# Two 64-row score products side by side, other head loads, and small moves in a decoder block's kernel

## The chip, the cores and the metric

The kernel runs on one core of one Trainium2 chip. The metric is the device time of one execution in microseconds (us); lower is better. It is a single launch with all arrays in the chip's memory; the largest part of the work is matrix products on TensorE (PE), with VectorE (DVE), ScalarE (ACT) and GpSimd (POOL) around it and transfers issued by SyncE (SP) and POOL.

## The reference

One decoder block with 1024 positions, width 1024 and FFN width 2816, in float32:

```python
h = rmsnorm(x, attn_norm_g)
z = h @ w_in                                  # u,v | pooled | q | k | v
gates = sigmoid(h @ w_gate + b_gate)          # three times 1024 columns
y_a = gmlp_mixer(z[..., :512])                # 256 wide
y_b = pool_mixer(z[..., 512:768])             # 256 wide
y_c = diff_attn_mixer(q, k, v, ...)           # 4 heads, values 128 wide
merged = g_a * (y_a @ proj_a) + g_b * (y_b @ proj_b) + g_c * (y_c @ proj_c)
x = x + merged @ w_out
x = x + conv_ffn(rmsnorm(x, ffn_norm_g), w_up, conv_w, conv_b, w_down)
return rmsnorm(x, final_norm_g)
```

The differential attention has, for each of its 4 heads, two maps with 64-wide queries and keys and one 128-wide value:

```python
s = einsum('bqhcd,bkhcd->bhcqk', qi, k) * scale + bias   # c: the two maps, d = 64
s = where(rel >= 0, s, -1e30)
p = softmax(s)
a = p[:, :, 0] - lam * p[:, :, 1]
o = einsum('bhqk,bkhd->bqhd', a, v)
```

## The kernel before

**Products.** Nearly every large product is made from operands split into a high and a low part (`hi`, `lo`, both fp32r), in three passes: hi x hi, hi x lo, lo x hi (`mm3`, L191, over `PASSES`). The projections, the output projection (`strassen_full`, in six products p = 0 to 5) and the FFN use a scheme of the Strassen and Winograd kind, which has fewer products and more additions (L262, L235, L888 and others on DVE).

**Order.** The program is written in stages, and generators (`filler`, `avs`, `nxt`, `lates`) are stepped by hand in the attention's main loop. A scheduler then orders each engine's instructions by their place in the program and by its own estimate of time; each engine runs its list in that order. Buffers come from pools: `wp` (`w4`, 13 buffers of 512 KB), `ap_` (`a4`, 34 buffers), `cp` (`c2`, 6 of half the size), and banks of PSUM from rings of 3 (scores, `score_bank`), 2 (`pat`), 1 (`pms`) and 2 (`pmm`).

**Stages in time.** x and the u and v columns to 55 us, values and pooling to 105, q and k to 195, twelve gate pairs to 430 and a last q and k pair to 446; then the attention to 592, the third merge to 632, the output projection to about 715, the FFN's norm and its first products to 765, its up part to 1120, its down part to 1380.

**Attention.** Each head has 8 query tiles of 128 rows, 32 steps in all; tile i needs the first (i + 1) x 128 keys, in chunks of at most 512. `store_qk` writes the split q and k of a head to memory (`qk_d`), `load_head` brings a head back: for each map c a buffer `qs` with the 64 rows of q's high part over the 64 rows of its low part, and `kh` and `kl`, each with the same 64 rows twice. `scores(t, c)` does one map: for each chunk one product of 128 rows with `kh` (L759) and one with `kl` (L760), which together are the passes hi x hi, lo x hi, hi x lo (and lo x lo); then DVE adds the bias and takes the row minimum (L762) and ACT takes the exponential (L768) with the minimum as bias. `transpose` (L1103), `attend` (L1112) and `sub_norm` (L1140) follow a few steps later. Between them stands filler: `merge_ab` (the merges of the first two mixers, L1146 for their weights `pr`, split into `ph`; L1165 and L1166 for the gates) and `merge_c`.

**Around it.** In the output projection `wfull` (L843) and `wh` (L835) load weights `fr`, DVE makes sums of them (L888), ACT and DVE split them into `fw` (L96, L97), ACT copies x (L912), and the result goes to memory at L1020. For the FFN's norm `rms4a` sums squares and takes a root by `rsqrt` on ACT (L123, a table has to be loaded for it) with one Newton step on DVE, `rms4b` broadcasts it. L390 makes the relative bias: it is the one place of the trunk where products use fewer than 128 rows (33).

Of the kernel before, what the change touches and what calls it, by code (L numbers as in the profile page):

```python
# [18 lines left out]
P = 128  # L19
# [3 lines left out]
NH = 512  # L23
# [24 lines left out]
def trunk_kernel(  # L48
# [446 lines left out]
    v_d = dram.tile([8, P, NH], F32, name="v_d")  # L495
# [6 lines left out]
    def values():  # L502
# [32 lines left out]
        def store(o, banks, c, r, i):  # L535

            for b in range(2):
                TT(out=o[b], in0=banks[b], in1=c[b], op=ALU.add)
                for t in range(2):
# [3 lines left out]
                nc.sync.dma_start(out=v_d[tt:tt + 2, :, r * 256:(r + 1) * 256].rearrange("t p c -> p t c"),  # L543
                                  in_=o[b].rearrange("p (t c) -> p t c", t=2))
# [132 lines left out]
    def store_qk(i, Fs, eng=None):  # L677
        for n_, F in enumerate(Fs):
# [6 lines left out]
            nc.sync.dma_start(out=qk_d[4 * n_ + i, 0], in_=hi.bitcast(F32))  # L685
            nc.sync.dma_start(out=qk_d[4 * n_ + i, 1], in_=lo.bitcast(F32))
# [20 lines left out]
    def load_head(hd):  # L707

        H = heads[hd] = dict(qkl=[])
# [15 lines left out]
        nc.sync.dma_start(out=H["V"], in_=v_d[:, :, hd * P:(hd + 1) * P].rearrange("t p c -> p t c"))  # L725
# [13 lines left out]
    def scores(t, c):  # L739
# [6 lines left out]
        if c == 0:  # L746
            if W <= NH:
                b = a4([P, 2, NH], n="sc")
                st[t] = dict(pr=[b[:, 0, :], b[:, 1, :]], s=[])
            else:  # L750
                st[t] = dict(pr=[a4(n="sc"), a4(n="sc")], s=[])
        q, kh, kl = H["qkl"][c]
        sc_ = st[t]["pr"][c]
        mx = tiny(2, "mx")
        chunks = [(0, min(NH, W))] + ([(NH, W - NH)] if W > NH else [])
        for n_, (c0, n) in enumerate(chunks):
            ps = score_bank[0]()
            qs = q[:, i * P:(i + 1) * P]
            nc.tensor.matmul(ps[:, :n], lhsT=qs, rhs=kh[:, c0:c0 + n], start=True, stop=False)  # L759
            nc.tensor.matmul(ps[:, :n], lhsT=qs, rhs=kl[:, c0:c0 + n], start=False, stop=True)  # L760
            o = (7 - i) * P + c0
            nc.vector.tensor_tensor_reduce(  # L762
                out=sc_[:, c0:c0 + n], in0=ps[:, :n], in1=H["T"][:, o:o + n], scale=1.0,
                scalar=mx[:, 0:1] if n_ else 3.0e38,
                op0=ALU.add, op1=ALU.min, accum_out=mx[:, n_:n_ + 1])
        nm_ = mx[:, n_:n_ + 1]
        sum_ = H["s0"][:, i:i + 1] if c == 0 else tiny(1, "s1")
        nc.scalar.activation(out=sc_[:, :W], in_=sc_[:, :W], func=AF.Exp, bias=nm_, scale=-1.0, accum_out=sum_)  # L768
        st[t]["s"].append(sum_)
# [39 lines left out]
    def strassen_full(src, w, nsl, x_d, out, done, tail=None, LL=4):  # L809
# [30 lines left out]
        def wfull(p, j):  # L840
            if (p, j) not in halves:
                t = w4(n="fr")
# [160 lines left out]
    tprep = [], []  # L1003
# [9 lines left out]
    def done1(d, j):  # L1013
# [47 lines left out]
        if (d // 4, j) == (1, 0):  # L1061
            tprep[1].append(t4)
# [14 lines left out]
    score_bank[0], pat, pms, pmm = pt2("sc", 3), pt2("at", 2), pt2("ms", 1), pt2("mm", 2)  # L1077
# [132 lines left out]
    mc = merge_c([pmm, pmm, *score_bank * 3, pat, pat])  # L1210
    lates = []
    for t in range(len(tiles) + 3):
        hd, i = tiles[min(t, 31)]
        if t == 0:
            yab = [load_yab(i) for i in range(4)]
        if t == 2:
            store_qk(NHEAD - 1, last_qk)
        if t % 8 == 3 and t < 24:
# [318 lines left out]
```

## Time and profile before

| | us |
|---|---|
| median of 3 runs | 1384.76 |
| lowest and highest run | 1382.77, 1390.9 |
| the profiled execution's own time | 1389.13 |
| its span in the trace | 1387.4 |
| its mean granted TensorE clock | 0.991 of full speed |

The profile records one execution of the program: every instruction of each engine with start and end, what it waited for, and every transfer. It is 4.4 us slower than the median of the runs, and its own time is 1.7 us more than its span. A matmul's recorded end is modelled, so the pace of PE is read from start to start. Engines other than PE have idle time that need not matter; what counts is where PE waits.

### The profile page before, as it was taken

Reading aid. Unit: us, or ns where it says so; the run is one execution under the profiler, and the core shown is the slowest. Engines: PE = TensorE matmul, PEld = TensorE weight load, DVE = VectorE, ACT = ScalarE, POOL = GpSimd, SP = SyncE. Lnnn points to the kernel's source line nnn. Section 1 sums busy time; section 2 is a strip of 40 time slices with the busy share of each in tenths; the row PEclk is TensorE's granted clock in tenths of the full one; section 3 lists DMA queues with packets and bytes.
Section 4 is the critical chain, followed back from the end, with each engine's and each line's share of the span. In section 5 each row is a group of like instructions: output and inputs, shape, how many; then the busy total and the mean of one; then the engine's idle time right before and its main releaser. Section 6 shows DMA issues by size and latency. Waiting matters only on the chain.

```text
span 1387.4 us, 17666 instructions
## 1 busy us (share of the span) xinstructions
PE 1344.9 (97%) x6454; PEld 1120.5 (81%) x6454; DVE 964.5 (70%) x1487; ACT 652.4 (47%) x1109; POOL 495.9 (36%) x327
## 2 busy tenths in 40 slices
PE   9999999999999989999999999999999999999997
PEld 7997778888887778877777888888888887878786
DVE  7985774445444879958769576666777669985853
ACT  8633343344433666723667343433343435455461
POOL 0022334455553000022221665666656640102014
PEclk9999999999999999999999999999999999999998
DMA  7023363333239898588795222212222248845853
GB/s 261 10 78 109 108 222 134 121 121 104 101 115 272 252 242 209 151 233 193 201 221 131 83 77 91 79 74 91 91 77 91 75 151 305 274 126 150 226 128 122
DMA packets 78831, 204.65 MB, mean 148 GB/s; under 512 B 8270, under 2 KB 17614, under 8 KB 78744
## 3 DMA queue, kind: packets, MB, share of 16 engines
q1 hardware_dynamic: 67224, 180.44, 39.4%
q0 software_dynamic: 11520, 23.07, 9.7%
q8 instruction: 51, 0.84, 0.2%
q14 instruction: 36, 0.29, 0.1%
HBM read 143.70 MB, written 47.46 MB: 138 GB/s over the span
## 4 chain that ended last, share of the span: by engine, by line
PE 67%; DVE 13%; DMA 10%; issue 6%; ACT 3%; POOL 1%; SPq 1%; DVEq 0%; POOLq 0%; ACTq 0%
PE b L191 59%; PE mm L191 2%; DMA fr<-in_w_down 2%; DMA pr<-in_w_proj 1%; DVE ft L97 1%; PE ms L1112 1%; DVE fw L97 1%; DMA qs<-qk_d 1%; POOL ga L104 1%; DMA fr<-in_w_out 1%; DVE sc L762 1%; DMA x<-in_xT 1%; DMA yr<-y_d 1%; PE sc L759 1%; ACT fw L96 1%
## 5 line engine op out<-in xcount | busy, mean ns | idle before, releaser
L191 PE MATMUL b<-ft,fw 128*128 128x512 f32 (+1 forms) x1308 | 293.0, 384 | 9.8 <-ACT x L912 3.4
L191 PEld LDWEIGHTS b<-ft,fw 128*128 128x128 f32 x1308 | 239.9, 189 | 60.3 <-DVE fw L97 4.0
L354 POOL TENSOR_TENSOR F<-F,RB 128x1024 f32<-128x1024 f32 x68 | 185.5, 2730 | 111.3 <-DVE F L262 110.2
L262 DVE TENSOR_TENSOR F<-b,c 128x512 f32<-128x512 f32 x152 | 100.9, 683 | 130.5 <-ACT c L281 58.3
L191 PE MATMUL b<-hb,Ah 128*128 128x512 f32 x608 | 190.2, 392 | 0.0
L191 PE MATMUL b<-T,Sh 128*128 128x512 f32 x504 | 155.8, 390 | 1.9 <-ACT c L272 1.9
L234 POOL TENSOR_TENSOR s<-r 128x512 f32<-128x512 f32 x36 | 54.4, 1512 | 224.3 <-DMA r<-in_w_up 84.2
L191 PEld LDWEIGHTS b<-hb,Ah 128*128 128x128 f32 x608 | 114.5, 189 | 24.0 <-issue 0.5
L191 PE MATMUL b<-hb,Al 128*128 128x512 f32 x304 | 119.5, 393 | 2.5 <-DVE Al L97 2.5
L97 DVE TENSOR_TENSOR Al<-r,Ah 128x1024 fp32r<-128x1024 f32 x38 | 56.1, 1476 | 94.0 <-issue 77.9
L97 DVE TENSOR_TENSOR Sl<-s,Sh 128x1024 fp32r<-128x1024 f32 x76 | 107.0, 1408 | 13.9 <-ACT Sh L96 8.5
L96 ACT CAST Sh<-s 128x1024 fp32r<-128x1024 f32 x76 | 80.0, 1052 | 75.6 <-PE b L191 43.2
L191 PEld LDWEIGHTS b<-T,Sh 128*128 128x128 f32 x504 | 94.6, 188 | 21.8 <-ACT c L272 2.4
L191 PE MATMUL b<-T,Sl 128*128 128x512 f32 x252 | 98.1, 389 | 0.0
L191 PE MATMUL b<-hb,Sh 128*128 128x512 f32 x304 | 94.1, 391 | 2.9 <-DVE F L262 2.9
L96 ACT CAST Ah<-r 128x1024 fp32r<-128x1024 f32 x38 | 39.9, 1049 | 110.9 <-PE b L191 104.0
L96 ACT CAST fw<-fr 128x512 fp32r<-128x512 f32 x90 | 54.8, 622 | 62.4 <-DVE fw L97 25.0
L191 PE MATMUL b<-Th,Sh 128*128 128x512 f32 x204 | 79.1, 391 | 0.8 <-ACT c L267 0.8
L191 PE MATMUL b<-Tl,Sh 128*128 128x512 f32 x204 | 79.5, 390 | 0.0
L191 PE MATMUL b<-Th,Sl 128*128 128x512 f32 x204 | 79.4, 389 | 0.0
L191 PEld LDWEIGHTS b<-hb,Sh 128*128 128x128 f32 x304 | 56.8, 188 | 16.6 <-DVE F L262 4.2
L191 PEld LDWEIGHTS b<-hb,Al 128*128 128x128 f32 x304 | 57.4, 189 | 15.3 <-DVE Al L97 2.9
(284 smaller groups left out, 2838.9 us busy)
## 6 DMA issues: line engine op xcount, KB each, us to landing
fr<-in_w_down SPq DMA_DIRECT2D x47, 512.0 KB, 3.8
r<-in_w_up SPq DMA_DIRECT2D x42, 512.0 KB, 3.5
r<-in_w_gate SPq DMA_DIRECT2D x24, 512.0 KB, 3.6
g_d<-F SPq DMA_DIRECT2D x24, 512.0 KB, 2.8
act_d<-cv SPq DMA_DIRECT2D x22, 512.0 KB, 2.8
act<-act_d SPq DMA_DIRECT2D x22, 512.0 KB, 7.8
fr<-in_w_out SPq DMA_DIRECT2D x18, 512.0 KB, 6.1
ssb<-sq POOLq DMA_DIRECT2D x24, 256.0 KB, 4.1
```

What stands on the lines that cost most here:

```text
L96: nc.scalar.copy(hi, src)
L97: (eng or nc.vector).tensor_tensor(out=lo, in0=src, in1=hi.bitcast(F32), op=ALU.subtract)
L104: nc.gpsimd.dma_start(out=dst, in_=src, accum_op=ALU.add)
L191: last_mm[0] = nc.tensor.matmul(ps, lhsT=w[a], rhs=x[b], start=first and i == 0, stop=last and i == 2, skip_group_check=more)
L234: eng.tensor_tensor(out=s1[:, :NH], in0=a21, in1=a22, op=ALU.add)
L262: nc.vector.tensor_tensor(out=o, in0=ps, in1=c, op=ALU.add)
L354: (eng or nc.gpsimd).tensor_tensor(out=F, in0=F, in1=RB, op=ALU.mult)
L759: nc.tensor.matmul(ps[:, :n], lhsT=qs, rhs=kh[:, c0:c0 + n], start=True, stop=False)
L762: nc.vector.tensor_tensor_reduce(out=sc_[:, c0:c0 + n], in0=ps[:, :n], in1=H["T"][:, o:o + n], scale=1.0, scalar=mx[:, 0:1] if n_ else 3.0e38,
L1112: nc.tensor.matmul(po[:, :P], lhsT=AH[t][:, kb, :], rhs=H["V"][:, kb, :], start=kb == 0, stop=kb == i)
```

## The change

It does these things:

- `scores(t, n_)` is called by chunk instead of by map. For a chunk it takes two score banks and writes, for each of the three passes, one product of 64 rows for each map: map 0 on the array's rows 0 to 63, map 1 on rows 64 to 127. There are 288 score products instead of 192. The bias, the minima and the exponentials stay as many. In the main loop both chunks stand one after the other ahead of the filler. Score banks become 4, `pmm` 1; `sub_norm`'s transposes use score banks.
- `load_head` loads q and k for both maps as they lie in memory (4 transfers of 128 x 1024), and V from rows that are now contiguous for a head; values are stored in that layout in twice as many transfers. A head's load starts one step later in each group of eight. The last head's `store_qk` moves from step 2 to step 5 and to POOL's queue. The filler starts at step 0, with the first merge's operands ahead of the y loads.
- `wfull` takes a buffer of the `a4` pool for product p = 3 of the output projection.
- For the FFN's norm, the four sums of squares that were called through `tprep` are called in `rms_mid`, both roots ahead of both broadcasts; the root is taken on DVE with three Newton steps and no operation on ACT.

```diff
-    def rms4a(sq, pool):
+    def rms4a(sq, pool, act=True):
...
-        return rsqrt(t, 4)
+        return rsqrt(t, 4, act)
...
-    v_d = dram.tile([8, P, NH], F32, name="v_d")
+    v_d = dram.tile([NHEAD, P, 8, P], F32, name="v_d")
...
-                nc.sync.dma_start(out=v_d[tt:tt + 2, :, r * 256:(r + 1) * 256].rearrange("t p c -> p t c"),
-                                  in_=o[b].rearrange("p (t c) -> p t c", t=2))
+                for k in range(2):
+                    nc.sync.dma_start(out=v_d[2 * r + k, :, tt:tt + 2, :],
+                                      in_=o[b].rearrange("p (t k c) -> p k t c", t=2, k=2)[:, k])
...
-    def store_qk(i, Fs, eng=None):
+    def store_qk(i, Fs, eng=None, queue=nc.sync):
...
-            q, kh, kl = (a4(dt=F32R, n=n) for n in ("qs", "kh", "kl"))
-            r = slice(64 * c, 64 * c + 64)
-            for dst, src in ((q[0:64], qk_d[hd, 0, r]), (q[64:128], qk_d[hd, 1, r]),
-                             (kh[0:64], qk_d[4 + hd, 0, r]), (kh[64:128], qk_d[4 + hd, 0, r]),
-                             (kl[0:64], qk_d[4 + hd, 1, r]), (kl[64:128], qk_d[4 + hd, 1, r])):
-                nc.sync.dma_start(out=dst.bitcast(F32), in_=src)
-            H["qkl"].append((q, kh, kl))
+            q, k = a4(dt=F32R, n="q"), a4(dt=F32R, n="k")
+            nc.sync.dma_start(out=q.bitcast(F32), in_=qk_d[hd, c])
+            nc.sync.dma_start(out=k.bitcast(F32), in_=qk_d[4 + hd, c])
+            H["q"].append(q)
+            H["k"].append(k)
...
-        nc.sync.dma_start(out=H["V"], in_=v_d[:, :, hd * P:(hd + 1) * P].rearrange("t p c -> p t c"))
+        nc.sync.dma_start(out=H["V"], in_=v_d[hd])
...
-        for n_, (c0, n) in enumerate(chunks):
-            ps = score_bank[0]()
-            qs = q[:, i * P:(i + 1) * P]
-            nc.tensor.matmul(ps[:, :n], lhsT=qs, rhs=kh[:, c0:c0 + n], start=True, stop=False)
-            nc.tensor.matmul(ps[:, :n], lhsT=qs, rhs=kl[:, c0:c0 + n], start=False, stop=True)
-            o = (7 - i) * P + c0
+        ps = [score_bank[0]() for _ in range(2)]
+        for k, (a, b) in enumerate(PASSES):
+            for c in range(2):
+                r = slice(64 * c, 64 * c + 64)
+                nc.tensor.matmul(ps[c][:, :n], lhsT=H["q"][a][r, i * P:(i + 1) * P], rhs=H["k"][b][r, c0:c0 + n],
+                                 start=k == 0, stop=k == 2)
...
-                t = w4(n="fr")
+
+                t = a4(n="fr") if p == 3 and nsl <= 4 else w4(n="fr")
...
-            tprep[1].append(t4)
+            t4s.append(t4)
...
-    score_bank[0], pat, pms, pmm = pt2("sc", 3), pt2("at", 2), pt2("ms", 1), pt2("mm", 2)
+    score_bank[0], pat, pms, pmm = pt2("sc", 4), pt2("at", 2), pt2("ms", 1), pt2("mm", 1)
...
-        if t == 2:
-            store_qk(NHEAD - 1, last_qk)
-        if t % 8 == 3 and t < 24:
+        if t == 5:
+            store_qk(NHEAD - 1, last_qk, queue=nc.gpsimd)
+        if t % 8 == 4 and t < 24:
             nxt = load_head(hd + 1)
-        if t % 8 >= 3:
+        if t % 8 >= 4:
             next(nxt, None)
         if t:
             scores(t, 0)
+            scores(t, 1)
         transpose(t - 2, 0)
         next(avs, None)
-        if t >= 1:
-            next(filler, None)
-        scores(t, 1)
+        next(filler, None)
+        if t == 0:
+            scores(t, 1)
...
     def rms_mid():
+        for n_, j in enumerate((1, 0)):
+            for f in t4s[2 * n_:2 * n_ + 2]:
+                f()
+            rs[j] = rms4a(stat[j], pb3, False)
+            yield
         for j in (1, 0):
-            rs[j] = rms4a(stat[j], pb3)
-            yield
             rms4b(rs[j], half(j), pb3)
             yield
```

The three places that follow show what stands in an engine's list before and after. The first is PE in the attention. `sc` is a score bank, `kh`, `kl` and `k` are moving keys, `qs` and `q` stationary queries; the numbers tell buffers apart. Before:

```order
L759 MATMUL sc_4118<-kh_3845,qs_3844 128x512
L760 MATMUL sc_4118<-kl_3846,qs_3844 128x512
L1112 MATMUL ms_4104<-V_3550,ah_4050 128x128 x4
L759 MATMUL sc_4122<-kh_3845,qs_3844 128x384
L760 MATMUL sc_4122<-kl_3846,qs_3844 128x384
L759 MATMUL sc_4138<-kh_3766,qs_3765 128x512
L760 MATMUL sc_4138<-kl_3767,qs_3765 128x512
L191 MATMUL mm_4109<-yv_3626,ph_4014 128x512
```
After, the same stage; `sc_4167` is the bank of map 0 and `sc_4168` that of map 1, and the two `k` and `q` are high and low parts:

```order
L191 MATMUL mm_4001<-yv_3641,ph_3755 128x512
L761 MATMUL sc_4167<-k_3843,q_3842 128x512
L761 MATMUL sc_4167<-k_3913,q_3842 128x512
L761 MATMUL sc_4167<-k_3843,q_3912 128x512
L761 MATMUL sc_4168<-k_3843,q_3842 128x512
L761 MATMUL sc_4168<-k_3913,q_3842 128x512
L761 MATMUL sc_4168<-k_3843,q_3912 128x512
L1118 MATMUL ms_4143<-V_3548,ah_4086 128x128 x4
L761 MATMUL sc_4177<-k_3843,q_3842 128x256
L761 MATMUL sc_4177<-k_3913,q_3842 128x256
L761 MATMUL sc_4177<-k_3843,q_3912 128x256
```
Where two products per map stood, three stand, and the maps come one after the other rather than in turns. In the list of after 36 of 48 chunks stand so; 11 stand in turns and one in part. One that stands in turns, the first chunk of the attention:

```order
L761 MATMUL sc_3665<-k_3524,q_3523 128x512
L761 MATMUL sc_3666<-k_3524,q_3523 128x512
L761 MATMUL sc_3665<-k_3530,q_3523 128x512
L761 MATMUL sc_3666<-k_3530,q_3523 128x512
L761 MATMUL sc_3665<-k_3524,q_3529 128x512
L761 MATMUL sc_3666<-k_3524,q_3529 128x512
```
Counted over the whole list, a product on one half of the rows stands next to one on the other half 66 times: 36 of 512 columns, 8 of 384, 13 of 256 and 9 of 128. The score products stand in 54 separate runs with other products between them; before there were 60 such runs, of which 37 followed an fp32 product (L1103, L1112) and 23 one of L191.

The second place is SP's list at the loading of the second head. Before:

```order
L716 DMA qs_3765<-qk_d 64x1024 x2
L716 DMA kh_3766<-qk_d 64x1024 x2
L716 DMA kl_3767<-qk_d 64x1024 x2
L722 DMA T_3774<-fsc 128x1024
L1165 DMA ga_3800<-g_d 128x1024
L1166 DMA gb_3801<-g_d 128x1024
L716 DMA qs_3844<-qk_d 64x1024 x2
L716 DMA kh_3845<-qk_d 64x1024 x2
L716 DMA kl_3846<-qk_d 64x1024 x2
L725 DMA V_3902<-v_d 128x8x128
L1165 DMA ga_4010<-g_d 128x1024
L1166 DMA gb_4011<-g_d 128x1024
L1146 DMA pr_4012<-in_w_proj 128x512
```
After:

```order
L713 DMA q_3842<-qk_d 128x1024
L714 DMA k_3843<-qk_d 128x1024
L721 DMA T_3846<-fsc 128x1024
L713 DMA q_3912<-qk_d 128x1024
L714 DMA k_3913<-qk_d 128x1024
L724 DMA V_3964<-v_d 128x1024
L1152 DMA pr_3994<-in_w_proj 128x512
```
The load has five transfers and V where there were thirteen and V, in larger pieces, and the gates' loads (`ga`, `gb`) no longer stand inside it; the projection weight `pr` comes right behind V in both.

The third is SP's list at the output projection, with product 3's weights at the `128x1024` rows and product 5's at `128x2x512`. Before:

```order
L843 DMA fr_6004<-in_w_out 128x1024
L843 DMA fr_6058<-in_w_out 128x1024
L1020 DMA x_d<-x_553_3611 128x512
L1020 DMA x_d<-x_554_3612 128x512
L1020 DMA x_d<-x_555_3613 128x512
L1020 DMA x_d<-x_556_3614 128x512
L843 DMA fr_6109<-in_w_out 128x1024
L843 DMA fr_6149<-in_w_out 128x1024
L835 DMA fr_6197<-in_w_out 128x2x512
L835 DMA fr_6245<-in_w_out 128x2x512
```
After:

```order
L849 DMA fr_6068<-in_w_out 128x1024
L1026 DMA x_d<-x_552_3611 128x512
L849 DMA fr_6122<-in_w_out 128x1024
L1026 DMA x_d<-x_553_3612 128x512
L849 DMA fr_6173<-in_w_out 128x1024
L1026 DMA x_d<-x_554_3613 128x512
L849 DMA fr_6213<-in_w_out 128x1024
L1026 DMA x_d<-x_555_3614 128x512
L840 DMA fr_6261<-in_w_out 128x2x512
```
Product 3's weights now stand between the stores of `x_d` instead of behind all four of them; the first of product 5's still stand behind.

## Rows read from the trace of the kernel before

**Rows 1.** The page: the span, and part 1, busy time of each engine.

```profile
span 1387.4 us, 17666 instructions
...
PE 1344.9 (97%) x6454; PEld 1120.5 (81%) x6454; DVE 964.5 (70%) x1487; ACT 652.4 (47%) x1109; POOL 495.9 (36%) x327
```

**Rows 2.** Windows: length; busy PE, PEld, DVE, ACT, POOL; clock, DMA share, GB/s.

```profile
446.70:500.00 53.30, 45.40 (x241) 36.80 (x241) 42.23 (x116) 31.81 (x85) 5.15 (x4) 0.94 0.94 269
500.00:592.00 92.00, 90.45 (x586) 79.35 (x584) 84.33 (x286) 65.53 (x202) 4.30 (x5) 1.00 0.76 191
```

**Rows 3.** Waits of PE, 440 to 600: total, times, longest.

```profile
PE mm L191 <- ACT ph L96: 3.3, 1, 3.3
PE sc L759 <- DVE mx L762: 2.5, 4, 1.5
PE sc L760 <- DMA kl<-qk_d: 1.6, 1, 1.6
```

**Rows 4.** Windows of 4 and 10 us, columns as in rows 2.

```profile
452.00:456.00 4.00, 4.00 (x12) 3.18 (x12) 4.00 (x11) 4.00 (x7) 0.37 (x1) 0.57 0.13 54
...
492.00:496.00 4.00, 2.63 (x7) 2.25 (x8) 2.13 (x8) 3.30 (x9) 0.00 (x0) 0.66 1.03 231
...
688.00:692.00 4.00, 3.62 (x10) 2.92 (x11) 1.95 (x3) 4.00 (x9) 3.25 (x5) 0.59 0.78 199
...
750.00:760.00 10.00, 8.19 (x40) 6.53 (x39) 10.00 (x18) 6.24 (x12) 2.18 (x3) 1.00 0.45 78
```

**Rows 5.** Matmuls of L759: ns min/median/max, first and last start, forms.

```profile
L759 PE MATMUL sc<-kh,qs x94: 220/389/522, 446.8 to 585.3; 128*128 128x512 f32 x46, 128*128 128x384 f32 x16, 128*128 128x256 f32 x16, 128*128 128x128 f32 x16
```

**Rows 6.** Timeline of PE, scores: start us, us, line, output and inputs.

```profile
480.75 0.39 PE L759 MATMUL sc<-kh,qs 128*128 128x512 f32 x1
...
481.43 0.39 PE L760 MATMUL sc<-kl,qs 128*128 128x512 f32 x1
...
488.99 0.42 PE L759 MATMUL sc<-kh,qs 128*128 128x384 f32 x1
489.25 0.34 PE L760 MATMUL sc<-kl,qs 128*128 128x384 f32 x1
489.42 0.39 PE L759 MATMUL sc<-kh,qs 128*128 128x512 f32 x1
...
507.89 0.28 PE L760 MATMUL sc<-kl,qs 128*128 128x128 f32 x1
508.00 0.34 PE L759 MATMUL sc<-kh,qs 128*128 128x256 f32 x1
...
508.29 0.28 PE L759 MATMUL sc<-kh,qs 128*128 128x256 f32 x1
508.41 0.28 PE L760 MATMUL sc<-kl,qs 128*128 128x256 f32 x1
```

**Rows 7.** Timeline of PE around L390 (33 rows), and its weight load behind.

```profile
130.32 0.39 PE L191 MATMUL b<-hb,Al 128*128 128x512 f32 x1
130.64 1.02 PE L390 MATMUL m<-oh,rb 33*4 33x512 f32 x2
131.59 0.73 PE L191 MATMUL b<-hb,Sh 128*128 128x512 f32 x2
132.15 0.40 PE L191 MATMUL b<-hb,Sl 128*128 128x512 f32 x1
...
131.59 0.30 PEld L191 LDWEIGHTS b<-hb,Sh 128*128 128x128 f32 x2 [0.86 <-issue]
```

**Rows 8.** Output projection: PE in the timeline; SP among the waits, 640 to 700.

```profile
688.38 2.08 PE L191 MATMUL b<-ft,fw 128*128 128x512 f32 x4 [3.36 <-ACT x L912]
...
SPq L835 <- DVE fw L97: 13.3, 3, 6.2
```

**Rows 9.** Timeline about the FFN norm: ACT and PE.

```profile
757.17 1.28 ACT L123 ACT_TABLE_LOAD   x1
...
760.14 0.73 PE L191 MATMUL b<-T,Sh 128*128 128x512 f32 x2 [1.95 <-ACT c L272]
```

More of the change, by code (lines that the diff above doesn't have):

```diff
@@ L684, in store_qk @@
                                            op0=ALU.mult, op1=ALU.subtract)
-            nc.sync.dma_start(out=qk_d[4 * n_ + i, 0], in_=hi.bitcast(F32))
-            nc.sync.dma_start(out=qk_d[4 * n_ + i, 1], in_=lo.bitcast(F32))
+            queue.dma_start(out=qk_d[4 * n_ + i, 0], in_=hi.bitcast(F32))
+            queue.dma_start(out=qk_d[4 * n_ + i, 1], in_=lo.bitcast(F32))
     def pool_outs():
@@ L707, in load_head @@
     def load_head(hd):
[L709 removed]
+        H = heads[hd] = dict(q=[], k=[])
         for c in range(2):
[L711 to L717 removed]
+            q, k = a4(dt=F32R, n="q"), a4(dt=F32R, n="k")
[3 more added lines that the diff above has]
+            H["k"].append(k)
             if c == 0:
@@ L737, in trunk_kernel, with scores @@
     score_bank = [pm1]
-    def scores(t, c):
+    def scores(t, n_):
         if t >= len(tiles):
@@ L745, in scores @@
         W = (i + 1) * P
-        if c == 0:
+        c0 = n_ * NH
+        n = min(NH, W - c0)
+        if n <= 0:
+            return
+        if n_ == 0:
+            st[t] = dict(s=[], mx=[tiny(2, "mx", 6) for _ in range(2)])
             if W <= NH:
                 b = a4([P, 2, NH], n="sc")
-                st[t] = dict(pr=[b[:, 0, :], b[:, 1, :]], s=[])
+                st[t]["pr"] = [b[:, 0, :], b[:, 1, :]]
             else:
-                st[t] = dict(pr=[a4(n="sc"), a4(n="sc")], s=[])
@@ L752, in scores @@
[L752 to L755, printed above, removed]
-        for n_, (c0, n) in enumerate(chunks):
-            ps = score_bank[0]()
-            qs = q[:, i * P:(i + 1) * P]
-            nc.tensor.matmul(ps[:, :n], lhsT=qs, rhs=kh[:, c0:c0 + n], start=True, stop=False)
-            nc.tensor.matmul(ps[:, :n], lhsT=qs, rhs=kl[:, c0:c0 + n], start=False, stop=True)
-            o = (7 - i) * P + c0
+                st[t]["pr"] = [a4(n="sc"), a4(n="sc")]
@@ L762, in scores @@
+        ps = [score_bank[0]() for _ in range(2)]
[4 more added lines that the diff above has]
+                                 start=k == 0, stop=k == 2)
+        o = (7 - i) * P + c0
+        for c in range(2):
+            sc_, mx = st[t]["pr"][c], st[t]["mx"][c]
             nc.vector.tensor_tensor_reduce(
-                out=sc_[:, c0:c0 + n], in0=ps[:, :n], in1=H["T"][:, o:o + n], scale=1.0,
+                out=sc_[:, c0:c0 + n], in0=ps[c][:, :n], in1=H["T"][:, o:o + n], scale=1.0,
@@ L764, in scores @@
                 scalar=mx[:, 0:1] if n_ else 3.0e38,
                 op0=ALU.add, op1=ALU.min, accum_out=mx[:, n_:n_ + 1])
[L766 to L769, printed above, removed]
+            if c0 + n == W:
+                sum_ = H["s0"][:, i:i + 1] if c == 0 else tiny(1, "s1")
+                nc.scalar.activation(out=sc_[:, :W], in_=sc_[:, :W], func=AF.Exp, bias=mx[:, n_:n_ + 1], scale=-1.0,
+                                     accum_out=sum_)
+                st[t]["s"].append(sum_)
@@ L1002, in trunk_kernel @@
     nc.scalar.mul(ngain, cs[:, C_GF:C_GF + KT], -1.0)
-    tprep = [], []
+    tprep, t4s = ([], []), []
     def op_g(src, g, n):
@@ L1209, in trunk_kernel @@
     LL = 4
-    mc = merge_c([pmm, pmm, *score_bank * 3, pat, pat])
+    mc = merge_c([pmm, *score_bank * 4, pat, pat])
     lates = []
@@ L1234, in trunk_kernel @@
         if u >= 0 and u % 8 == 7 and u < 31:
-            lates.append(sub_norm(tiles[u][0], (0, 1), pmm))
+            lates.append(sub_norm(tiles[u][0], (0, 1), score_bank[0]))
         if u == 27:
-            lates.append(sub_norm(3, (1,), pmm))
+            lates.append(sub_norm(3, (1,), score_bank[0]))
         if 0 <= t - 2 < 32:
```

1 line of the change is left out of this document (added).

## The prediction

> **What bounds the kernel now.** I read part 1 of the page first: PE is busy 1344.9 of 1387.4 us [rows 1]. So nearly everything that adds work to PE adds time, and other engines matter only where PE waits for them. The windows then say where PE has slack. In the first part of the attention (446.7 to 500) PE is busy 45.40 of 53.30 us at a mean clock of 0.94; in the rest of it (500 to 592) 90.45 of 92.00, at full clock [rows 2]. The waits name the idle time of the first part: 3.3 us for ACT's split of a projection weight (ph L96), 2.5 us for DVE's row minima (mx L762), 1.6 us for a half of a head that is still being loaded (kl<-qk_d) [rows 3]. The DMA share there is 1.03 in 492 to 496 [rows 4]: the queue engines are full, so the weights that ACT splits are late because the loads of a head stand in front of them. Twice in this part, and once in the output projection, PE's granted clock falls: 0.57, 0.66 and 0.59 of full speed in windows of 4 us [rows 4], the latter two right behind waits of 3.3 and 3.36 us [rows 3, 8]. At the lower of the two levels (1.2 instead of 2.4 GHz) a mean of 0.57 over 4 us is about 3.4 us of half pace, which loses 1.7 us.
>
> **A. The score products themselves.** L759 ran 96 times (94 in the row, and two under another bank's name) and L760 as often: per map and chunk one product each, 48 of 512 columns and 16 each of 384, 256 and 128 [rows 5]. From start to start they take 0.2265 us for 512 columns (480.75 to 481.43, three products), 0.17 for 384 (489.25 to 489.42), 0.12 for 256 (508.29 to 508.41) and 0.11 for 128 (507.89 to 508.00) [rows 6]. That is 2 x (48 x 0.2265 + 16 x 0.17 + 16 x 0.12 + 16 x 0.11) = 34.5 us.
> The change needs three products per map and chunk where two did, since hi and lo of q no longer stand over each other: 288 for 192. Had they to run one after another: 34.5 x 1.5 = 51.8, or +17.3. Were each product hidden beside one of the other map: 51.8 / 2 = 25.9, or -8.6. Which of the two is decided by who is whose neighbour. The built order shows that the maps seldom alternate: of 48 chunks 36 stand as three passes of one map and then three of the other, because the second map's bank is waited for, and only 11 alternate, one more in part. PE is taken to start them in the order in which they stand; then a product can lie beside another only if that one uses the other 64 rows and stands next to it, and there are 66 such pairs of neighbours (36 of 512, 8 of 384, 13 of 256, 9 of 128): 36 x 0.2265 + 8 x 0.17 + 13 x 0.12 + 9 x 0.11 = 12.1 us hidden at best. So 51.8 - 12.1 = 39.7: **+5**, bounds -8.6 and +17.3.
>
> **B. The array's shape.** Before, all the attention's products use 128 rows. Now 54 separate runs of score products of 64 rows stand between products of 128 rows, and each enters and leaves another shape of the array. One place in the trace shows such a change: L390, 33 rows among L191's 128 [rows 7]. The last product before it starts at 130.32 and L390 at 130.64, 0.32 later, where 0.226 is the pace: 0.09 lost on entering. Its two products start at 130.64 and, with 0.427 each in that pace (their 1.02 less the pipeline's 0.16), the last one ends its streaming at about 131.50. The first L191 that streams normally stands at 132.15, the third of its run, so the run would have begun at 132.15 - 2 x 0.226 = 131.70; its weight load started only at 131.59, after PEld had idled 0.86, instead of beside the product before. That is 0.21 on leaving; together 0.30 per run, 54 x 0.30 = 16.2. Of the old 60 runs 37 come from an fp32 group, and the first product then takes 0.26 until the next where 0.17 is the pace (488.99 to 489.25 to 489.42) [rows 6]: 37 x 0.085 = 3.1 that is paid already. Net **+13**, an estimate from one place with another row count; bounds 0 (a change of shape that no weight load has to wait for) and +18.
> The Trainium skill says so too ("TensorEngine Tiling (Array Packing)", Key Properties): to change the tiling mode drains TensorE. The row agrees, with 0.30 per run; the page gives no figure for it. The same page lets tiles on different rows work in parallel and prices a contraction of 64 at up to two times (Theoretical Speedup); by that price A would be -8.6 and the sum -7, where the order and the row make it +7. No row of before shows two products at once.
>
> **C. Waits of the attention's first part.** A head is now loaded by 5 large transfers and V, 3 MB in place of 4 (k is no longer loaded twice), from whole rows; it starts one step later in each group of eight. The last head's store moves from step 2 to step 5 and from SP's queue to POOL's, where nothing in this part is waited for. With a quarter of a head's bytes gone and head 1's V ahead of the third projection weight as before, that weight's wait (3.3) and the low clock behind it (1.7) should go, and the wait for kl (1.6): -6.6. The four waits for the minima (2.5) and the first low-clock stretch (1.7) may go with the fourth score bank and with filler from step 0: -10.8 at the outside. The mm bank that is given up costs little, since the merge products take turns with scores. I take **-7**, bounds 0 (the weight is late all the same) and -11.
>
> **D. The output projection.** PE waits 3.36 us at 688.38 for ACT's x, and SP stood 13.3 us behind DVE for w4 buffers [rows 8]: loads of w_out come late because the few w4 buffers are still held by splits. Product 3's loads now use the larger a4 pool, and in the order four of them move ahead of or between the x1 stores. But product 5's loads still stand after the stores and still take w4. The wait and its low-clock stretch are 3.4 + 1.7 = 5; I take **-4**, bound 0.
>
> **E. The FFN norm's root.** The ACT table load of 1.28 us (757.17) goes, and with it a cause of PE's 1.95 us wait for ACT's c at 760.14 [rows 9]. In its place DVE gets nine small operations of some 0.17 us in a stretch where it is busy 10.00 of 10 us [rows 4], ahead of the broadcast that PE waits for. The T4 product's sums are called elsewhere in the code but stand where they stood on DVE. **0**, bounds -2 and +1.5.
>
> **F. The rest.** V's store takes 16 transfers with 512-byte pieces in place of 8 with 1 KB, while the qk products keep PE busy; the load of V gets whole rows of 4 KB. 0 to +1 if the smaller pieces delay weights; taken at nothing. ab(0) ahead of the y loads is hidden behind the last gate pair.
>
> **Sum:** +5 +13 -7 -4 = +7 on the profiled execution's 1389.13, thus 1396; that execution stands 4.4 above the median of the runs, so **1392 us**, with 1385 to 1399 as this case's own range (B between 0.2 and 0.4 per run, C and D between half and all).
>
> **Rivals.**
> 1. The shape changes cost next to nothing. A run of K = 64 might load its weights ahead as others do; L390 has 33 rows and 4 columns, and is one place. Then +5 -7 -4, up to -10 with all of C and D whole (5 - 11 - 5 = -11): 1374 to 1379. It decides from under 0.1 us per run. For it: PE is 97% busy with PEld at 81% [rows 1], so weights are loaded beside products everywhere else. Against it: PEld's 0.86 of idleness in [rows 7]. I put 1376 (1368 to 1381).
> 2. No product lies beside another at all: +17.3 with B and the gains, 17 + 13 - 11 = +19: 1404. For it: no row of before shows two products at once. Against it: nothing but that the two halves share neither rows nor banks.
> 3. The maps do run side by side in spite of the order, because a product may begin on its rows as soon as these are free: -8.6, with a small B and the gains: 1366. Against it: the three passes of one map come first, and the other's bank is waited for.
> This kernel's runs spread from 1382.8 to 1390.9, so under 0.5% (6.9 us) counts as no change.
>
> **How the numbers follow.** Forecast 0.42, rival 1 0.30, rival 2 0.18, rival 3 0.10. Faster is under 1377.8: rival 3 whole, some 0.8 of rival 1: 0.34. Slower is over 1391.7: rival 2 and half of the forecast: 0.39. Same: the rest, 0.27. The range is 1364 to 1406, from rival 3 to rival 2's middle.
>
> **What would show it.** B: the scores' first product and the first L191 or fp32 product behind a run lie more than 0.2 us beyond the pace, with PEld idle ahead of them. A: products of the other map start much sooner than 0.2 us after their neighbour, 66 times; if more, rival 3. C: no wait for ph and no window under 0.9 clock in 480 to 500. D: the L912 wait is under 1 us. It would be wrong if PE's idle time inside 500 to 592, now 1.55 us, grew: then the bank waits have become the bound.

## The result and the profile after

The changed kernel takes 1397.78 us (median of 6 runs, 1394.22 to 1400.07), the kernel before 1385.49 (6 runs): a ratio of 1.0087, 95% interval 1.0069 to 1.0105, so 12 us slower. The profiled execution of after took 1397.29, at its median; the one of before (1389.13) lay 3.6 above its own. The two traces therefore differ by 8.2 us of span only, and a cause worth 4 us can't be read from them alone. Of these 8.2 us 2.9 lie ahead of the attention: the first score product of all starts at 436.67 before and at 439.53 after (timeline of PE, before and then after):

```profile
436.67 0.39 PE L759 MATMUL m<-kh,qs 128*128 128x512 f32 x1
```

```profile
439.53 0.50 PE L761 MATMUL m<-k,q 64*128 64x512 f32 x2
```

Some 1.7 of them (0.28 x 6) are a stretch at the lower clock. Windows of before and then after, columns as in [rows 2]:

```profile
84.00:90.00 6.00, 5.94 (x48) 5.91 (x49) 4.20 (x5) 2.88 (x5) 0.00 (x0) 1.00 0.00 0
```

```profile
84.00:90.00 6.00, 5.34 (x32) 5.34 (x33) 3.06 (x4) 0.80 (x2) 0.00 (x0) 0.72 0.00 0
```

In the same window the experiment e3 below has 0.72 too and e8 1.00, though both share with after all that runs there. So this stretch comes and goes with the execution and is no part of the change's price.

The page of after, its span and part 1, beside [rows 1]:

```profile
span 1395.6 us, 17830 instructions
...
PE 1358.9 (97%) x6550; PEld 1120.4 (80%) x6550; DVE 968.0 (69%) x1499; ACT 651.8 (47%) x1106; POOL 501.0 (36%) x331
```

PE is busy 14 us longer, and the span grew by 8.2: PE's work rose, and some of its waits went. Windows of after, columns as in [rows 2]:

```profile
446.70:500.00 53.30, 51.07 (x309) 38.19 (x310) 50.38 (x141) 38.12 (x96) 9.27 (x8) 1.00 0.87 294
500.00:592.00 92.00, 92.00 (x587) 71.44 (x586) 76.19 (x248) 58.66 (x179) 4.36 (x5) 1.00 0.48 141
642.00:692.00 50.00, 44.58 (x189) 36.47 (x188) 44.13 (x73) 25.60 (x46) 10.58 (x12) 0.93 0.78 200
770.00:776.00 6.00, 4.44 (x17) 3.97 (x18) 5.16 (x15) 0.59 (x1) 2.54 (x2) 0.72 0.24 97
```

The first part of the attention is now 51.07 of 53.30 us busy, at full clock: it was 45.40 at 0.94. The second part is full. But the clock is 0.93 in 642 to 692, 0.07 x 50 x 2 = 7 us at the lower level, and low again at 770 to 776. The waits of PE, 440 to 780, say why (total, times, longest):

```profile
PE b L191 <- DVE gc L1210: 5.4, 1, 5.4
PE b L146 <- DVE rs L131: 2.5, 1, 2.5
...
PE at L1109 <- DVE sc L1094: 0.7, 1, 0.7
```

All of [rows 3] is gone, and so are the waits of PE for ACT's x and for ACT's c in [rows 8, 9]. In their place stand 5.4 us at the start of the output projection, for the last products of the third merge that DVE has yet to take out of their banks (gc), and 2.5 us at the FFN norm's broadcast, for its root on DVE. The score products, beside [rows 5]:

```profile
L761 PE MATMUL sc<-k,q x282: 218/387/503, 450.2 to 590.5; 64*128 64x512 f32 x72, 64*128 64x128 f32 x24, 64*128 64x256 f32 x23, 64*128 64x384 f32 x22
```

With six more under another bank's name they are the 288 that the order shows. Around a run of them PE's timeline reads so:

```profile
453.43 0.49 PE L191 MATMUL mm<-yv,ph 128*128 128x512 f32 x1
453.85 1.04 PE L761 MATMUL sc<-k,q 64*128 64x512 f32 x6
455.38 0.73 PE L191 MATMUL mm<-yv,ph 128*128 128x512 f32 x2 [0.48 <-DVE yv L97]
456.04 1.03 PE L761 MATMUL sc<-k,q 64*128 64x256 f32 x6
```

One product of L191 between two runs of scores takes 0.42 us from start to start (453.43 to 453.85) where 0.2265 is the pace. The change of the array's shape has a price here, as at L390 [rows 7].

### The profile page after: what moved, and what is told of

It is laid out like the page before. It is cut to its first block, busy times and chain, and to the rows that moved or that the text cites. A ratio compares the mean times of both kernels' runs of the same rounds, so it can differ in the third digit from the quotient of the medians.

```text
span 1395.6 us, 17830 instructions
## 1 busy us (share of the span) xinstructions
PE 1358.9 (97%) x6550; PEld 1120.4 (80%) x6550; DVE 968.0 (69%) x1499; ACT 651.8 (47%) x1106; POOL 501.0 (36%) x331
## 5 line engine op out<-in xcount | busy, mean ns | idle before, releaser
L191 PE MATMUL b<-ft,fw 128*128 128x512 f32 (+1 forms) x1308 | 292.7, 384 | 9.4 <-DVE gc L1210 5.4
L191 PEld LDWEIGHTS b<-ft,fw 128*128 128x128 f32 x1308 | 240.3, 189 | 59.3 <-issue 5.8
L191 PE MATMUL b<-hb,Ah 128*128 128x512 f32 x608 | 190.2, 392 | 0.0
L191 PE MATMUL b<-T,Sh 128*128 128x512 f32 x504 | 155.8, 390 | 0.0
L191 PEld LDWEIGHTS b<-hb,Ah 128*128 128x128 f32 x608 | 114.7, 189 | 24.2 <-issue 0.5
L191 PE MATMUL b<-hb,Al 128*128 128x512 f32 x304 | 119.3, 393 | 2.5 <-DVE Al L97 2.5
L97 DVE TENSOR_TENSOR Sl<-s,Sh 128x1024 fp32r<-128x1024 f32 x76 | 108.0, 1422 | 14.0 <-ACT Sh L96 7.1
L97 DVE TENSOR_TENSOR Al<-r,Ah 128x1024 fp32r<-128x1024 f32 x38 | 54.6, 1438 | 90.2 <-issue 76.0
L191 PEld LDWEIGHTS b<-T,Sh 128*128 128x128 f32 x504 | 94.5, 188 | 19.6
L191 PE MATMUL b<-T,Sl 128*128 128x512 f32 x252 | 98.1, 389 | 0.0
L191 PE MATMUL b<-hb,Sh 128*128 128x512 f32 x304 | 94.1, 391 | 3.5 <-DVE F L262 3.5
L191 PE MATMUL b<-Th,Sh 128*128 128x512 f32 x204 | 79.0, 390 | 0.8 <-ACT c L267 0.8
L191 PE MATMUL b<-Tl,Sh 128*128 128x512 f32 x204 | 79.4, 389 | 0.0
L191 PE MATMUL b<-Th,Sl 128*128 128x512 f32 x204 | 79.4, 389 | 0.0
L191 PEld LDWEIGHTS b<-hb,Sh 128*128 128x128 f32 x304 | 56.8, 188 | 17.3 <-DVE F L262 4.8
L191 PEld LDWEIGHTS b<-hb,Al 128*128 128x128 f32 x304 | 57.5, 189 | 15.3 <-DVE Al L97 2.9
```

The source lines that it names most:

```text
L97: (eng or nc.vector).tensor_tensor(out=lo, in0=src, in1=hi.bitcast(F32), op=ALU.subtract)
L191: last_mm[0] = nc.tensor.matmul(ps, lhsT=w[a], rhs=x[b], start=first and i == 0, stop=last and i == 2, skip_group_check=more)
```

## The experiments

All ratios are to the kernel before, run on the same chip, with 95% intervals. Medians of runs that went together can be subtracted; e1 to e4 went together, e5, e6, e8 and e9 did, and e10 to e12 did.

### Where the scores' time goes: e1, e2, e3

**e1: two passes over 128 rows.** Each score mixes the two maps and lacks a pass; the work on the other engines is the same.

```diff
-        for k, (a, b) in enumerate(PASSES):
+        for k, (a, b) in enumerate(PASSES[:2]):
...
-                r = slice(64 * c, 64 * c + 64)
+                r = slice(0, P)
```

> The changed kernel with its score products over all 128 rows and two passes instead of three: 192 products as before, no change of the array's shape, everything else as in the changed kernel. Each score then mixes both maps and lacks the third pass, so the attention's numbers are others. Theory (the shape changes cost 0.39 us per run and the overlap only pays the third pass): 1397.8 - 20 = about 1378 (1373 to 1383). Rival (the scores are neutral, and the 5.4 us wait ahead of the output projection with the low clock behind it make the loss): 1394 or more if that wait stays.

Measured: 1380.04 us, 0.9941 (0.9928 to 0.9954). The scores cost all of the loss and more: without them the change gains 8 us. The wait for gc stayed (6.1 us), so the rival is out.

**e2: three passes over 128 rows.** 288 products one after another, no change of shape.

```diff
-                r = slice(64 * c, 64 * c + 64)
+                r = slice(0, P)
```

> The same with three passes over 128 rows: 288 products, none beside another, no change of shape; each score mixes both maps. Theory: 1397.8 - 21 (53 runs at 0.39) + 17 (the overlap that is lost) = about 1394 (1389 to 1399). Rival (a shape change costs next to nothing, the overlap is what counts): 1415. Against the run with two passes: +17.3.

Measured: 1394.67 us, 1.0050 (1.0035 to 1.0065). The third pass costs 14.6 us over e1. The two intervals allow 12 to 18, so this isn't told apart from the 17.3 of its pace.

**e3: both maps on rows 0 to 63.** Map 1 is computed from map 0's queries and keys.

```diff
-                r = slice(64 * c, 64 * c + 64)
+                r = slice(0, 64)
```

> The changed kernel with both maps' products on rows 0 to 63: as many products, the same shape changes, but no two can lie beside each other; map 1 is computed from map 0's queries and keys. Theory from the trace of after (products overtake each other, so that some 17 us lie beside others): 1415 (1411 to 1419). The prediction's step A (only neighbours in the order, 12.1 us): 1410. No overlap on the chip at all: 1398.

Measured: 1415.21 us, 1.0202 (1.0186 to 1.0219), as the theory from the trace has it. Against e2 the number of products and nearly the order are the same, and neither has two beside each other; what differs is the shape. So **the shape changes cost 1415.2 - 1394.7 = 20.5 us**, by the two intervals give or take 3, or 0.38 for each of 54 runs. The same place of the program shows it, in e2 and then in e3 (timeline of PE):

```profile
450.57 0.39 PE L191 MATMUL mm<-yv,ph 128*128 128x512 f32 x1
450.80 1.55 PE L761 MATMUL sc<-k,q 128*128 128x512 f32 x6
452.19 0.63 PE L191 MATMUL mm<-yv,ph 128*128 128x512 f32 x2
```

```profile
454.54 0.49 PE L191 MATMUL mm<-yv,ph 128*128 128x512 f32 x1
454.96 1.65 PE L761 MATMUL sc<-k,q 64*128 64x512 f32 x6
456.54 0.73 PE L191 MATMUL mm<-yv,ph 128*128 128x512 f32 x2
457.21 0.98 PE L761 MATMUL sc<-k,q 64*128 64x256 f32 x6
```

In e2 the product of L191 takes 0.23 from start to start and the run of six 1.39 (450.80 to 452.19); in e3 0.42 and 1.58. That is 0.19 more in the one and 0.19 more in the other, 0.38 together. Where in them it lies is shown by the second product of the run at 454.96 and the second of the pair at 456.54, each by itself in e3's timeline:

```profile
455.30 0.39 PE L761 MATMUL sc<-k,q 64*128 64x512 f32 x1
```

```profile
456.88 0.40 PE L191 MATMUL mm<-yv,ph 128*128 128x512 f32 x1
```

Each change of shape lengthens two steps. The step across it, from the last product of the old shape to the first of the new, is 0.33 where 0.23 is the pace (456.88 to 457.21); the next one, from the first product of the new shape to its second, is 0.34 (454.96 to 455.30, and 456.54 to 456.88). The Trainium skill's "TensorEngine Tiling (Array Packing)" (Key Properties) says that changing the mode drains TensorE; these rows agree and give the price.

Against after, e3 lacks only the overlap: 1.0202 - 1.0087 of 1386 is **15.9 us that the pairs hide**, again give or take 3. The stretch from the first score product in a bank `sc` (a few ran earlier, under another bank's name) to the first product of the output projection says the same. In after, e3, e2 and e1 (windows, columns as in [rows 2]):

```profile
450.22:651.40 201.18, 193.69 (x1131) 151.39 (x1131) 162.31 (x464) 112.26 (x313) 25.64 (x28) 0.99 0.69 202
```

```profile
450.51:667.57 217.06, 210.75 (x1131) 166.31 (x1131) 163.75 (x464) 112.69 (x314) 25.62 (x28) 1.00 0.64 185
```

```profile
446.79:646.15 199.36, 192.38 (x1132) 167.26 (x1130) 163.17 (x463) 111.89 (x313) 25.84 (x28) 1.00 0.69 204
```

```profile
448.17:633.27 185.10, 177.31 (x1037) 151.79 (x1036) 159.24 (x463) 111.52 (x313) 25.85 (x28) 0.99 0.75 221
```

217.06 - 201.18 = 15.9 for the overlap, 199.36 - 185.10 = 14.3 for the third pass. For the shape it is 217.06 - 199.36 = 17.7. Ahead of the stretch e3 is 3.7 us later than e2 (450.51, 446.79): two earlier runs of scores stand there, and the low clock at 85 us, which isn't the shape's. So the 20.5 may hold up to 2 us that aren't the shape's.

15.9 is more than the 12.1 that neighbours in the order can hide. PE's busy time in L761 alone says so without the spread of the runs; in after and then e3 (windows of that line: length; busy PE, PEld; clock, DMA share, GB/s):

```profile
430.00:610.00 180.00, 48.76 (x288) 29.74 (x288) 1.00 0.64 206
```

```profile
430.00:610.00 180.00, 66.47 (x288) 45.21 (x288) 1.00 0.56 180
```

That is 17.7 us less for the same 288 products. The trace of after shows how. In its timeline and, for the first tenth of a microsecond of the second of these runs, among the instructions of L761:

```profile
491.52 0.63 PE L761 MATMUL sc<-k,q 64*128 64x256 f32 x6
```

```profile
L761 PE MATMUL sc<-k,q x2: 437/466/494, 513.5 to 513.5; 64*128 64x512 f32 x1, 64*128 64x384 f32 x1
```

The run at 491.52 is the one of 256 columns that the order begins with three products of sc_4177; three of sc_4178 follow them there. The six take 0.63 us here, and six such take 0.98 in e3 (the row at 457.21): three pairs run, though the order has one pair of neighbours. At 513.5 PE's list reads

```
L761 MATMUL sc_4444<-k_3843,q_3842 128x512
L761 MATMUL sc_4444<-k_3913,q_3842 128x512
L761 MATMUL sc_4444<-k_3843,q_3912 128x512
L761 MATMUL sc_4497<-k_3843,q_3842 128x384
```

and a product of 384 columns starts in the same tenth of a microsecond as the first of 512: it went past two that stand ahead of it and wait for the other half of the rows. It doesn't always happen: the six of 256 columns at 456.04 (timeline above) take 1.03 us, no less than in e3. In PE's list the second map's first product waits for DVE there; that its bank was not yet free is the likely reason. "TensorE: Matmul & The Clock Gate" (Part 3) of the Trainium skill has products start strictly in program order; this run shows otherwise for products on different rows.

### Which parts give, which take: e4, e5, e6, e8

**e4: the new scores alone**, with their loads of q and k, banks and order; v_d, the loop's steps, store_qk's queue, wfull and rms_mid as before. Of the change it has this, and the new scores whole:

```diff
-            q, kh, kl = (a4(dt=F32R, n=n) for n in ("qs", "kh", "kl"))
+            q, k = a4(dt=F32R, n="q"), a4(dt=F32R, n="k")
...
-    score_bank[0], pat, pms, pmm = pt2("sc", 3), pt2("at", 2), pt2("ms", 1), pt2("mm", 2)
+    score_bank[0], pat, pms, pmm = pt2("sc", 4), pt2("at", 2), pt2("ms", 1), pt2("mm", 1)
```

> The kernel before with the new scores alone: 64-row products, their q and k loads, banks and place in the loop; the values' layout, the step of the head loads, the last head's store, the output projection's buffers and the norm's root are as before. Theory (the scores cost +20, and the other parts give back some 8): 1385.5 + 20 = about 1404 (1399 to 1409), less what the smaller q and k loads save in waits. Rival (the scores are neutral, the other parts lose): 1386.

Measured: 1396.73, 1.0064 (1.0050 to 1.0077). It is slower alone, but by 9 where e1 to e3 price the products at 19, and below the expected range: some 10 us come back with the scores' own order, banks and loads. What else the change has adds nothing to that: after stands at 1.0087, and the two intervals overlap.

**e5: the norm as before.**

```diff
-            rs[j] = rms4a(stat[j], pb3, False)
+            rs[j] = rms4a(stat[j], pb3)
...
-            t4s.append(t4)
+            tprep[1].append(t4)
```

> The changed kernel with the FFN norm as before (root on ACT, sums of squares called where they were). The prediction's step E says 0. The trace of after says that the root on DVE makes PE wait 2.5 us at the broadcast instead of 0.3 there and 1.9 for ACT's c, and that a stretch of half clock (1.7 us lost) follows: about 2 us faster than the changed kernel, 1.000 to 0.997 of it, so 1.006 to 1.009 of the kernel before.

Measured: 1397.54, 1.0076 (1.0052 to 1.0100); the intervals overlap with after's, so the 2 us are not resolved. In its waits the 2.5 us at the broadcast are 0.3 again, and the 1.7 for ACT's c are back.

**e6: product 3's weights in the old pool.**

```diff
-                t = a4(n="fr") if p == 3 and nsl <= 4 else w4(n="fr")
+                t = w4(n="fr")
```

> The changed kernel with product 3's weights of the output projection in the old pool. The prediction's step D says that this costs 4 us (the wait for ACT's x comes back). The rival: the buffers only moved the wait to the start of the projection, where PE now waits 5.4 us for DVE's gc and then runs 6.8 us at half clock; then that wait goes and the kernel is 3 to 7 us faster than the changed kernel, 1.004 to 1.007 of the kernel before. If the wait for gc stays, it comes from the loads or the banks.

Measured: 1400.80, 1.0111 (1.0095 to 1.0126), some 3 us slower than after by the two ratios, whose intervals overlap. The waits of PE, 600 to 700:

```profile
PE b L191 <- DVE gc L1210: 5.4, 1, 5.4
PE b L191 <- ACT x L918: 0.2, 1, 0.2
```

The wait for gc stays, and the old wait for ACT's x doesn't come back: neither theory named what the buffers are worth. In e4, which has the old buffers too and none of the moves of the loads, that wait is short as well, and there is none for gc (waits of PE, 440 to 780):

```profile
PE b L191 <- ACT x L917: 0.5, 1, 0.5
```

So the old wait goes without the buffers.

**e8: the moves of the loads undone** (head loads from step 3, store_qk at step 2 on SP, filler from step 1, no early ab(0)).

```diff
-        if t == 5:
-            store_qk(NHEAD - 1, last_qk, queue=nc.gpsimd)
-        if t % 8 == 4 and t < 24:
+        if t == 2:
+            store_qk(NHEAD - 1, last_qk)
+        if t % 8 == 3 and t < 24:
```

> The changed kernel with the head loads, the last head's store, the filler and the first merge's operands at their old steps of the loop (q, k and V still in the new layout). The prediction's step C gives these moves and the smaller loads 7 us together. If the moves matter, 3 to 5 us slower than the changed kernel (1.011 to 1.013 of before), and the wait for gc ahead of the output projection shrinks since PE comes there later; if the smaller loads were all of it, the same as the changed kernel (1.009).

Measured: 1395.09, 1.0067 (1.0053 to 1.0081): not slower, so no gain of the moves shows; the wait for gc shrinks as expected. Its waits of PE, 600 to 700, and then DVE's longest waits in after, 592 to 652:

```profile
PE mm L191 <- DVE gb L1185: 0.8, 1, 0.8
PE b L191 <- DVE gc L1210: 0.6, 1, 0.6
```

```profile
DVE ga L880 <- DMA ga<-gc: 9.4, 4, 5.9
```

The end of the third merge and the first product of the output projection, in e8 and in after (timeline of PE):

```profile
646.33 2.88 PE L191 MATMUL sc<-yc,ph 128*128 128x512 f32 x12
649.04 1.30 PE L191 MATMUL b<-ft,fw 128*128 128x512 f32 x5
```

```profile
643.10 2.88 PE L191 MATMUL sc<-yc,ph 128*128 128x512 f32 x12
651.40 1.62 PE L191 MATMUL b<-ft,fw 128*128 128x512 f32 x3 [5.42 <-DVE gc L1210]
```

With the moves PE comes to the merge's last group 3.2 us sooner (643.10, 646.33), and leaves it 2.4 us later (651.40, 649.04): the wait for gc is 0.6 without them and 5.4 with them. In after DVE stood 9.4 us before that for merged blocks (ga) to land, and 3.2 in e8; in its timeline the output projection's sums (L880 to L883) and splits (L97) stand between the gc operations. The stretch from the first score product in a bank `sc` to the output projection, 201.18 us in after, is in e8 (windows)

```profile
448.32:649.05 200.73, 196.81 (x1132) 153.28 (x1132) 155.79 (x451) 106.87 (x308) 22.16 (x23) 0.99 0.64 189
```

**The gain of the moves in the attention is given back at the next stage's door.**

### Without the pairs: e9 to e13

**e9: the old products and their loads of q and k, all else of the change.**

```diff
+        for k in range(2):
+            for c in range(2):
+                x = H["qkl"][c]
+                nc.tensor.matmul(ps[c][:, :n], lhsT=x[0][:, i * P:(i + 1) * P], rhs=x[1 + k][:, c0:c0 + n],
+                                 start=k == 0, stop=k == 1)
```

> The changed kernel with the old scores' products (q's high over low part, two products of 128 rows) and their loads of q and k, 4 MB per head; by chunk, with the new banks and all else of the change. The run with two passes (0.9941 of before) has the same PE work with 3 MB. If bytes don't matter any more behind the other moves: 1379 to 1381 (0.994). If the smaller loads were what freed the attention: 1385 to 1388 (0.998 to 1.000), with a wait for q, k or ph back.

Measured: 1384.56, 0.9988 (0.9970 to 1.0007), between the two. The first part of the attention in e9 and in e1 (windows):

```profile
446.70:500.00 53.30, 49.00 (x286) 40.03 (x285) 50.98 (x146) 38.60 (x100) 8.23 (x8) 1.00 1.04 304
```

```profile
446.70:500.00 53.30, 51.63 (x309) 42.66 (x308) 51.20 (x150) 39.12 (x103) 9.31 (x8) 1.00 0.89 309
```

With 4 MB per head the DMA share is 1.04 and PE busy 49.00; with 3 MB 0.89 and 51.63. The bytes cost PE some 2.6 us there. The ratios lie 0.47%, 6.5 us, apart, and all of it lies in the stretch up to the output projection, which is 185.10 in e1 and in e9 (windows)

```profile
446.92:638.50 191.58, 178.89 (x1037) 151.92 (x1036) 159.90 (x464) 111.70 (x314) 25.56 (x28) 0.99 0.84 231
```

1.0 of it is a longer wait for gc at its end (7.1 for 6.1).

**e10: e9 with the norm as before.**

```diff
-            rs[j] = rms4a(stat[j], pb3, False)
+            rs[j] = rms4a(stat[j], pb3)
```

> The run with the old products and loads of q and k, and now the FFN norm as before too. There the trace shows PE waiting 3.2 us for the norm's sums and then 6.8 us at half clock. If these come from the norm's new place: 3 to 5 us faster than that run, 0.995 to 0.997 of before. If they are only where the lateness of the projection shows: the same, 0.999.

Measured: 1382.40, 0.9985 (0.9967 to 1.0003): the same as e9. If the norm's new place is worth anything, it is less than these intervals resolve.

**e11: e10 with the moves of the loads undone.**

```diff
-            store_qk(NHEAD - 1, last_qk, queue=nc.gpsimd)
-        if t % 8 == 4 and t < 24:
+            store_qk(NHEAD - 1, last_qk)
+        if t % 8 == 3 and t < 24:
```

> The same with the head loads, the last store, the filler and the first merge's operands at their old steps. What is left of the change: the order by chunk, the banks, the values' layout and product 3's buffers. With 64-row products these moves were worth nothing, since PE then waits for DVE's gc ahead of the output projection. If that holds here too: the same as the run with them. If the old products have the larger loads to hide: 3 to 6 us slower, 1.000 to 1.003 of before.

Measured: 1380.40, 0.9951 (0.9933 to 0.9970): faster than before, and the moves are worth nothing here either, though its waits for kh and ga (2.5 us each) are there. Among the versions that keep all passes of the scores its ratio is the lowest, but e12 and e13 lie within its interval.

**e12: e10 with the head loads alone back at step 3.**

```diff
-        if t % 8 == 4 and t < 24:
+        if t % 8 == 3 and t < 24:
```

> The run without the new norm, with only the head loads back at the third step of eight (the other moves stay). With 4 MB per head the load has a step more to land: if PE's waits for gates of the first merges (2.2 us) come from a load that is too dense, 1 to 3 us faster than at the fourth step; if not, the same.

Measured: 1380.31, 0.9965 (0.9946 to 0.9984), 2 us under e10, and the two intervals overlap: inconclusive.

**e13: order and banks alone.** Everything as before but scores by chunk for both maps, four score banks, one merge bank and sub_norm in score banks.

```diff
-    score_bank[0], pat, pms, pmm = pt2("sc", 3), pt2("at", 2), pt2("ms", 1), pt2("mm", 2)
+    score_bank[0], pat, pms, pmm = pt2("sc", 4), pt2("at", 2), pt2("ms", 1), pt2("mm", 1)
```

> The kernel before with one thing of the change: scores by chunk, both maps after one another in four score banks, one merge bank, the sub-norm's transposes in score banks. Products, loads, values' layout, buffers and norm are as before. If the order and the banks make what the last three runs gained: 0.995 to 0.997 of before. If product 3's buffers or the values' layout make it: 0.999 to 1.001, and PE's wait for ACT's x of 3.4 us is there again.

Measured: 1380.48, 0.9966 (0.9947 to 0.9984): this part by itself makes about all that e11 has. Its waits of PE, 440 to 780:

```profile
PE sc L762 <- DVE F L262: 2.8, 1, 2.8
PE mm L191 <- DVE ga L1186: 2.3, 3, 1.0
...
PE b L191 <- ACT x L919: 1.8, 1, 1.8
```

The wait for ph (3.3) of [rows 3] is gone with the loads as they were, and of that for the minima (2.5) 0.2 are left; the wait for a load of q or k stays (1.6, now for kh), a new one for DVE's F has come (2.8), and none for gc. The wait for ACT's x, 3.36 in [rows 8], is 1.8: it moves with whatever comes ahead of it.

## Why the prediction was right, and which of its steps were not

The sum was +7 on the profiled execution; the traces differ by 8.2 and the medians by 12. The forecast case was the right one: A and B together were +18, and the runs make them 14.6 + 20.5 - 15.9 = +19. That the two agree is in part luck: A was 6 us too high and B 7.5 too low. C to F were -11 and came to 12 - 19 = -7 (e1, the change without the price of its scores, gains 8); this is the larger part of the 6 us by which the time lies above the forecast of 1392.

- **Step A failed in its rule.** "PE is taken to start them in the order in which they stand; then a product can lie beside another only if that one uses the other 64 rows and stands next to it" gave 12.1 us of overlap. The runs show 15.9 (e3 against after), and the busy time 17.7, since a product goes past others that wait for the other half of the rows (rows at 491.52 and 513.5). With the third pass at 14.6 for 17.3, A is -1.3 instead of +5. Rival 3 had this mechanism, but not its limit: pairs whose bank is waited for stay apart, and the price of the shape remains.
- **Step B was mis-sized.** The mechanism holds: 0.38 per run, not 0.30, and no 3.1 us to take off: 20.5 instead of 13. Leaving came out about as read (0.21). On entering, the step across the change is 0.10 longer, as at L390 (0.09); but the step behind it is 0.11 longer too, and the prediction took L390's as that product's own pace. The 3.1 us were read from one step alone. In before the L1112 group ahead of the row at 488.99 [rows 6] reads

```profile
488.18 1.05 PE L1112 MATMUL ms<-V,ah 128*128 128x128 f32 x8
```

  At 0.11 each (the step of products of 128 columns) the eighth starts at 488.95, and the score product stands only 0.04 behind it: it starts about as much too soon as its own step then loses (0.26 for 0.17).
- **Step C was right about the waits.** [Rows 3] are empty in after, and the attention's clock is 1.00. e1 has the stretch from the first score product in a bank `sc` to the output projection at 185.10 us; in before the same stretch reads (windows)

```profile
446.75:639.79 193.04, 183.09 (x1038) 154.71 (x1037) 154.03 (x455) 109.67 (x311) 21.45 (x23) 0.98 0.83 221
```

  so it is 7.9 shorter, in spite of 6.1 us of a new wait in it. About 5 of the 7 us that I gave to the loads come with the order by chunk and the banks alone (e13, whose interval allows 2 to 7).
- **Step D failed in its mechanism.** "I take -4" supposed that the wait for ACT's x goes for good, and by product 3's buffers. It went, but in e6 and e4 it is 0.2 and 0.5 with the old buffers, so its sign (under 1 us) came true and proved nothing. And PE now waits 5.4 us for gc, at the start of the same stage, with some 7 us of lower clock behind it, worth 3.5. e8 ties that wait to the moves of the loads, and e6 shows that the buffers don't cause it; by e6 they are worth 3 us, give or take 3, from what is left open.
- **Step E** at 0 stands within what the runs resolve (e5, e10); its trace shows a wait of 1.9 exchanged for one of 2.5 and a low clock (0.72 in 770 to 776). **Step F** at 0: nothing in the runs speaks against it.
- Rival 1 (shape changes for nothing) and rival 2 (no overlap) are both excluded by e3, which is slower than e2 by 20.5 and slower than after by 15.9.

The kernels with the old products say of the moves what e8 says. The same stretch in e10 and e12, with moves, and in e11 and e13, without (windows):

```profile
447.22:636.85 189.63, 179.89 (x1037) 151.86 (x1036) 158.36 (x463) 111.31 (x313) 25.99 (x28) 0.99 0.85 233
```

```profile
443.84:632.76 188.92, 177.58 (x1037) 151.89 (x1036) 160.36 (x464) 112.62 (x314) 25.50 (x28) 0.99 0.86 234
```

```profile
445.93:634.61 188.68, 178.86 (x1037) 153.42 (x1036) 155.52 (x456) 109.31 (x312) 22.03 (x23) 0.99 0.82 227
```

```profile
447.05:634.38 187.33, 179.63 (x1038) 154.57 (x1036) 155.67 (x456) 109.01 (x312) 22.13 (x23) 0.98 0.84 228
```

They lie within 2.3 us of each other, though e10 and e12 end with a wait for gc of 5.8 and 7.0 us and the other two with none: what the moves save in the attention is about that wait. Three of these traces (e10, e12, e13) lie 3 to 4 us below their kernels' medians, so that 1 or 2 us between them mean nothing.

## What to carry to other kernels

Two 64-row products side by side save, against two stacked passes of 128 rows, only 4 x 0.2265 - 3 x 0.2265 = 0.23 us per chunk of 512 columns, and every run of them between 128-row products costs 0.38 (e3 against e2): here a run needs two full chunks to break even, and 48 chunks stood in 54 runs. Count the runs in the built order before counting the products. And where a stage ends in another engine's backlog, time won ahead of it is waited for at the stage's end: look at what the next stage's first product needs, before moving loads.

## What the runs showed of the hardware

- Products on different rows pass each other in PE's list: a product of 384 columns started in the same tenth of a microsecond as one of 512 that stands three places ahead of it, with two between.
- Two products on different rows run side by side at almost no cost to each other: six products of 256 columns take 0.63 us as three pairs and 0.98 on one half, and the 288 score products keep PE busy for 48.76 us in after and for 66.47 on one half (e3).
- A change between 64 and 128 rows costs some 0.2 us, half in the step across it (0.33 for 0.23, 456.88 to 457.21 in e3) and half in the next step (0.34 for 0.23, 454.96 to 455.30 and 456.54 to 456.88).
